# W_ada in bursts of four: regrouping the second part of a modulation inside a transformer block kernel

## The chip, the cores and the metric

The kernel runs on one core of a Trainium2 chip. The metric is the device time of one execution in microseconds, the median of several runs. Five engines work side by side in one core: PE (TensorE, matrix products; its weight loads are listed as PEld), DVE (VectorE), ACT (ScalarE), POOL (GpSimd) and SP (SyncE, which here issues every DMA). Each engine executes its own instructions in a fixed order, and they wait for each other through semaphores.

## The reference, cut to what matters

One block of a network over 1024 tokens of width 1024: a modulation, attention with dilated branches, a gated delta rule, an output projection, a feed-forward part and a last norm. The change touches the modulation alone, one row vector times a 1024x6144 matrix:

```python
c_act = jax.nn.silu(c)
mod = c_act @ w_ada[l] + b_ada[l]
sh1, sc1, g1, sh2, sc2, g2 = [m[:, None, :] for m in jnp.split(mod, 6, axis=-1)]
h = _rmsnorm(x, norm_attn_g[l]) * (1.0 + sc1) + sh1
...
x = x + g1 * y
h = _rmsnorm(x, norm_ffn_g[l]) * (1.0 + sc2) + sh2
...
x = x + g2 * y
```

sh1 and sc1, the first third, are needed at once, and the kernel computes them in its first stage. g1, sh2, sc2 and g2, the last two thirds, are not needed before the output projection. They are columns 2048 to 6143 of W_ada, 16 MB, and they are what the change is about.

## The kernel before, in words

**Stages.** First the norm, the first third of the modulation and six column blocks of the input projection (lines 156 to 500). Then the gated delta rule for two groups of four heads (`delta(0)`, `delta(1)`, lines 1165 to 1193), then attention (`attend`, 1310), the output projection (`out_delta`, 1335, and the loop at 1463), the feed-forward part and the last norm. The large products are made of three matmuls on numbers split in a high and a low part, 128x128 weights against 512 or 256 columns.

**Filler.** The delta rule is a chain of small steps that pass between PE, DVE, ACT and POOL. So that PE has work meanwhile, the rest of the input projection is a generator, `others()` (1106): each `yield` stands for a group of three matmuls and names their estimated time (0.64 or 0.32 us, lines 572 and 595). `turn(name)` (556) pulls as much filler as the table FILL (42) says ahead of a step; `until(...)` and `hold(...)` (1139 to 1147) pull until a named projection is done. `mixed()` (1126) wraps the generator: when more than MODS = 1.9 us of filler have gone by, and the flag `quiet` is not set (it is, in the triangular inverse of a group, line 943), it advances the modulation by one step.

**The modulation's last two thirds.** `modulation()` (1084) is a generator too. It goes through eight column groups `i` of 512 columns. For each of the eight row blocks `k` of 128 rows it takes a tile `wm` of 128x512 (256 KB), loads it from W_ada (1094), and calls `rows4` (191), which issues four matmuls: the column `cc[:, k:k+32]` as weights of 32 columns, and 128 strided columns of the tile as moving data, each into its own 32 partitions of the PSUM bank `mods`. In the records each of these four matmuls stands as two, so one tile is `x8` in a view. A column group takes a quarter (128 columns) of the bank; after its eight tiles, `by_columns` (201) lets DVE transpose the quarter into a tile `mt` (204) and add the bias into `mod` (208). The matmuls accumulate on what lies in the bank (`start=False`), so DVE clears the whole bank before group 0 and before group 4 (1090). There are 64 tiles in all, and a `yield` after each.

**Slots.** The tiles `wm` share the tag `tc` with two other users: `Rs`, three tiles in the first microseconds (183), and `tc_` in the triangular inverse (887), with TCB = 3 slots for all. A tile can be loaded when the tile that held the slot before is done with. The tiles `mt` share the two slots of the tag `zt` with the outputs of the z projection (612).

**Order.** The order of each engine's instructions is made by a planner before the run: it takes, on each engine, the instruction with the lowest place in the program among those whose inputs and slots are there by its own estimate. `urgent()` (93) puts an instruction 6000 places ahead; the loads of `wm` are written that way, as are the loads of the projection weights (`wsplit`, 210).

Of the kernel before, what the change touches and what calls it, by code (L numbers as in the profile page):

```python
# [10 lines left out]
F32 = mybir.dt.float32  # L11
# [7 lines left out]
P = 128  # L19
T = 1024  # L20
D = 1024
KT = D // P
TB = T // P
HALF = 512
# [2 lines left out]
SKEW = 4  # L27
TCB = 3
MODS = 1.9
EARLY = 1  # L30
LEVELS = ("qd", 4), ("z1", 36)
TAIL = 4
# [38 lines left out]
def build(tc, I, out):  # L71
    nc = tc.nc
# [3 lines left out]
    def pool(name, side="left", bufs=1, space=None):  # L76
        st = ExitStack()
        kw = {} if space is None else {"space": space}
        p = st.enter_context(
            tc.tile_pool(name=name, bufs=bufs, side=side, reuse_waits="tile", **kw)  # L80
        )
        return p, st
# [7 lines left out]
    def const(shape, name, dt=F32):  # L90
        return cp.tile(shape, dt, name=name, tag=name)

    def urgent():
        return tc.high_priority(offset=6000)
# [26 lines left out]
    pd, sd = pool("pd")  # L121
# [9 lines left out]
    def psb(name, tag, bufs):  # L131
        return pg.tile([P, HALF], F32, name=name, tag=tag, bufs=bufs)

    def gbank(name):
        return psb(name, "g", 2)
# [4 lines left out]
    def tbank(name):  # L140
        return psb(name, "t", 2)

    def abank(name):
        return psb(name, "a", 1)

    def ybank(name):
        return psb(name, "y", 1)

    def start(name, tag, shape=None, dt=F32):

        n = {"xp": 2, "qk": 4, "lu": 5, "o": 2, "VN": 2, "R": 1, "tc": TCB, "yt": 1, "os": 1, "zl": 1}.get(tag, 2)
        return pd.tile(shape or [P, T], dt, name=name, tag=tag, bufs=n)
# [3 lines left out]
    cc = const([P, KT + 31], "cc")  # L156
# [20 lines left out]
    for j in range(3):  # L177
        n = min(HALF, 1152 - HALF * j)
        ps = tbank(f"ps_R{j}")
# [11 lines left out]
    def rows4(ps, win, w, nt, last):  # L191

        v = w.rearrange("p (t j m) -> p j t m", j=4, m=32)
        for j in range(4):
            nc.tensor.matmul(
                ps[32 * j : 32 * j + 32, 0 : 32 * nt], win, v[:, j], start=False, stop=last, skip_group_check=True
            )

    def by_columns(ps, out, nt, add=None, shape=None, tag="os"):

        t = shape or start("turned", tag, [P, 256])
        nc.vector.transpose(t[:, 0 : 32 * nt], ps[:, 0 : 32 * nt])
        if add is None:
            nc.vector.tensor_copy(out, t[:, 0 : 32 * nt : 32])
        else:
            nc.vector.tensor_tensor(out=out, in0=t[:, 0 : 32 * nt : 32], in1=add, op=ALU.add)
# [207 lines left out]
    for i in range(2):  # L416
        ps = aux[:, P * i : P * i + P]
# [126 lines left out]
    def ahead(us):  # L544

        some = us > 0
        while us > 0:
            w = next(fill[0], None)
            if w is None:
                break  # L550
            us -= w
            used[0] += w
        return some and last[0] is not None
# [44 lines left out]
    def run(gen):  # L598
        for _w in gen:
            pass  # L600


    for q in range(2):
        ps = gbank(f"g_qd{q}")
# [478 lines left out]

    def modulation():
        pm = ybank("mods")
        for i in range(8):
            t0 = 16 + 4 * i
            ps = pm[:, P * (i % 4) : P * (i % 4 + 1)]
            if i % 4 == 0:
                nc.vector.memset(pm, 0.0)  # L1090
            for k in range(KT):
                w = pd.tile([P, HALF], F32, name=f"wm_{i}_{k}", tag="tc", bufs=TCB)
                with urgent():
                    nc.sync.dma_start(w, I["wada"][k * P : (k + 1) * P, t0 * P : t0 * P + HALF])
                rows4(ps, cc[:, k : k + 32], w, 4, k == KT - 1)
                yield
            t = pv.tile([P, 256], F32, name=f"mt{i}", tag="zt", bufs=2)
            by_columns(ps, mod[:, t0 : t0 + 4], 4, bada[:, t0 : t0 + 4], shape=t)
        nc.vector.scalar_tensor_tensor(
            out=G2, in0=mod[:, 32:40], scalar=1.0, in1=gff, op0=ALU.add, op1=ALU.mult  # L1100
        )

    done = set()
    mods = modulation()

    def others():
        def group1(which):
            for i, (kind, col) in enumerate((("kd", KD), ("qd", QD), ("vd", VD))):
                if kind in which:
                    for q in range(2):  # L1110
                        yield from proj_d(col + 2 + q, f"{kind}{2 + q}", spill(f"{kind}{q}", _.pj[2 * i + q]))
                    done.add(kind)

        yield from proj_t(I["wz0"], 256, "z0", z_evac(0))
        yield from group1(("kd", "qd", "vd"))
        yield from proj_t(I["wz1"], 256, "z1", z_evac(1))
        done.add("z1")
        for hp in range(4):
            if hp < 2:
                yield from proj_t(I["wva"][hp], 256, f"va{hp}", va_end(hp))  # L1120
                done.add(f"va{hp}")
            for col, kk in ((KA, 4), (QA, 0)):
                yield from proj_d(col + hp, f"a{kk}_{hp}", spill(f"a{kk}_{hp}", _.qk[kk + hp]))
            done.add(hp)

    def mixed():

        t = 0.0
        for c in others():
            yield c  # L1130
            t += c
            if t > MODS and not quiet[0]:
                t = 0.0
                next(mods, None)

    quiet = [False]
    fill[0] = mixed()

    def hold(what, us):
# [5 lines left out]
    def until(ready):  # L1145
        while not ready():
            used[0] += next(fill[0])
# [17 lines left out]
    def delta(g):  # L1165
        st = {}
        kt = []
        for j in range(4):
            kind, q = ("k", j) if j < 2 else ("q", j - 2)
            hp = 2 * g + q  # L1170
            t = pd.tile([P, T], F32, name=f"{kind}d{hp}", tag=f"{kind}d", bufs=2)
            (kd if kind == "k" else qd)[hp] = t
            if g == 0:
                conv((4 if kind == "k" else 0) + hp, xps[j], t)
                kt.append(delta_turn(g, kind, q, t, norms=norms[0], keep=kind == "k"))
                if j == 1:
                    nc.scalar.activation(norms[0]["lr"], norms[0]["rk"], AF.Ln, bias=eps1)
            else:
                nc.sync.dma_start(t, _.cv[j])
                if kind == "k":  # L1180
                    kt.append(delta_turn(g, kind, q, t, keep=True))
        delta_prep(g, st, norms[g], kt[0:2], delta_rows(g))
        if g == 1:
            until(lambda: "vd" in done)
        delta_v(g, st, [lambda q=q: vxp[q] if g == 0 else fetch(4 + q, f"v{2 + q}") for q in range(2)])
        delta_inverse(g, st)
        until(lambda: ("qd", "z1")[g] in done)
        delta_scan(g, st)
        if g == 0:
            delta_early()  # L1190

    delta(0)
    delta(1)
    until(lambda: EARLY - 1 in done)
    run(mods)
# [90 lines left out]
    def att_value(hp, qb, ets):  # L1286
# [12 lines left out]
        if qb % 4 == 3:  # L1299
            cs = slice((qb - 3) * P, (qb + 1) * P)  # L1300
            if hp < EARLY:
                t = pa.tile([P, HALF], F32, name=f"yo{hp}_{qb}", tag="xo", bufs=3)
# [7 lines left out]
    def attend(switch):  # L1310
        units = [(hp, qb) for hp in range(4) for qb in range(TB)]
        xs, ets = {}, {}
        for i in range(len(units) + AV):
            if i >= AV and units[i - AV] == (EARLY, 3):
                switch()
            if i < len(units):
                hp, qb = units[i]
                if hp not in loaded:
                    until(lambda: hp in done)
                    loaded[hp] = att_load(hp)  # L1320
                if i < EARLY * TB + 3 + AV:
                    ahead((FRONT - used[0]) / (EARLY * TB + 3 + AV - i))
                if qb >= 2 and hp < 3 and hp + 1 in done and hp + 1 not in loaded:
# [35 lines left out]
    def switch():  # L1359

        run(fill[0])
        sh_.close()
        p1_, st1 = pool("py", side="right")
        p2_, st2 = pool("pyd", side="right")
        closing.extend((st1, st2))
        for k in range(KT):
            p_ = p1_ if k < 4 else p2_
            yh[k] = p_.tile([P, T], F32R, name=f"yh{k}", tag=f"yh{k}")
            yl[k] = p_.tile([P, T], F32R, name=f"yl{k}", tag=f"yl{k}")
        for k in range(4, 8):  # L1370
            y_load(k, _.yd[k // 2 - 2][k % 2])
        fill[0] = out_delta()
# [3 lines left out]
    sy, syd = closing  # L1376
    for k in range(EARLY):
        y_load(k, _.ya[k])
    run(fill[0])

    ps = abank("g2t")
# [81 lines left out]
    for hf in range(2):  # L1463
# [4 lines left out]
        for d in range(KT):  # L1468
            slabs = [(wsplit(I["wo"][d, 0], 512, f"wo{d}_0_{hf}"), 0)]
            t = x2[d, hf]  # L1470
            nc.sync.dma_start(t, _.xp[2 * d + hf])
            ps = (gbank, sbank)[d % 2](f"wo{d}_0_{hf}")
# [204 lines left out]
    for k in range(4):  # L1677
# [3 lines left out]
        t = px.tile([P, HALF], F32, name=f"t2_{k}", tag="m", bufs=5)  # L1681
# [232 lines left out]
```

## Time and profile before

| what | value |
|---|---|
| median of 3 runs | 1443.23 us (1440.9 to 1454.74) |
| the profiled execution's own time | 1445.04 us |
| its span, from the first to the last instruction | 1443.3 us |
| PE busy in the span | 95% |
| DVE, ACT, POOL busy | 61%, 46%, 21% |
| mean granted clock of PE | 0.985 |
| loads of `wm`, line 1094 | 64 of 256 KB |

A row of the profile's groups or of its timeline names the time, the engine, the line of the kernel, the operation, the tile that is written, the tiles that are read, and the shape; `x8` counts instructions that follow each other. A matmul row shows its weights as `128*32` (rows and columns of the array) and its moving data as `128x128`. Matmuls are pipelined, and the ends of their bars are modelled: what one costs is read from the distance between starts. In brackets stands how long the engine was idle ahead of it and what ended that. A view by windows gives the busy time of each engine in a stretch of the span, with the granted clock of PE (PEclk, 1.00 is full) and what DMA moved.

### The profile page before, as it was taken

How to read it: one execution, taken by the hardware profiler on the slowest of the kernel's cores; microseconds unless marked ns; L12 is line 12 of the kernel's file. 1: busy time of each engine (PE TensorE's matmuls, PEld its weight loads, DVE VectorE, ACT ScalarE, POOL GpSimd, SP SyncE). 2: the span in 40 equal slices, each digit the busy share in tenths (PEclk: the TensorE clock that was granted, in tenths of full speed). 3: DMA queues.
4: the chain of work that ended last, by engine and by line, in shares of the span. 5: the costliest groups of instructions: out<-in, count | busy, mean ns of one | idle time of the engine just before them, and what ended most of it. 6: DMA issues, size and time to landing. Idle time of an engine off the chain costs nothing.

```text
span 1443.3 us, 24528 instructions
## 1 busy us (share of the span) xinstructions
PE 1372.5 (95%) x8984; PEld 1112.9 (77%) x8984; DVE 875.8 (61%) x1660; ACT 668.3 (46%) x1283; POOL 310.3 (21%) x279
## 2 busy tenths in 40 slices
PE   7998989997999699999998989999999999999997
PEld 4776857787879677777876868888888888888885
DVE  3587762665746223376426997757576776474487
ACT  3487523348233345576337743333333333444456
POOL 1345412243333334454244300000000000000000
PEclk9998999999999999999999999999999999999999
DMA  8736464466541643651375445636354565766666
GB/s 300 244 119 172 139 197 148 148 183 185 156 121 45 190 109 103 187 147 67 127 229 163 147 137 177 204 108 211 124 182 144 163 217 183 265 213 202 194 222 234
DMA packets 171921, 245.69 MB, mean 170 GB/s; under 512 B 33078, under 2 KB 76391, under 8 KB 171800
## 3 DMA queue, kind: packets, MB, share of 16 engines
q1 hardware_dynamic: 171800, 244.12, 54.4%
q8 instruction: 71, 1.16, 0.4%
q14 instruction: 50, 0.41, 0.1%
HBM read 181.30 MB, written 67.48 MB: 172 GB/s over the span
## 4 chain that ended last, share of the span: by engine, by line
PE 58%; DVE 6%; DMA 4%; ACT 2%; issue 1%; POOL 1%; SPq 0%; DVEq 0%; ACTq 0%; POOLq 0%
PE wua L1536 8%; PE wga L1536 8%; PE X L1731 6%; PE g_a L570 5%; PE wuc L1536 4%; PE Z L1731 4%; PE wgc L1536 4%; PE wo L570 3%; PE y L1295 2%; PE Y L1731 2%; PE tr L1278 2%; PE wgb L1536 2%; PE wub L1536 2%; PE g_va L593 2%; PE S L1254 1%
## 5 line engine op out<-in xcount | busy, mean ns | idle before, releaser
L1526 DVE TENSOR_TENSOR wl_db<-wr_db,wh_db 128x512 fp32r<-128x512 f32 x77 | 53.2, 691 | 76.4 <-ACT wh_db L1525 76.2
L1525 ACT CAST wh_db<-wr_db 128x512 fp32r<-128x512 f32 x77 | 47.9, 622 | 98.7 <-PE X L1731 41.3
L1258 DVE CUSTOM_DVE_ANT_0 X<-S,ng 128x512 f32<-128x512 f32 (+3 forms) x64 | 36.7, 587 | 71.5 <-PE S L1255 58.4
L1263 ACT ACTIVATE X<-X,sc 128x128 f32<-128x128 f32 (+7 forms) x64 | 49.4, 773 | 42.0 <-DVE sc L1258 36.6
L1731 PE MATMUL X<-wl_db,wh_da 128*128 128x512 f32 x176 | 68.6, 390 | 0.2 <-DVE wl_db L1526 0.2
L1731 PE MATMUL X<-wh_db,wh_da 128*128 128x512 f32 x176 | 68.6, 390 | 0.0
L1731 PE MATMUL X<-wh_db,wl_da 128*128 128x512 f32 x176 | 68.5, 389 | 0.0
L1265 POOL TENSOR_SCALAR X<-X,sc 128x128 f32<-128x128 f32 (+7 forms) x64 | 49.9, 782 | 82.3 <-DVE sc L1264 80.8
L1526 DVE TENSOR_TENSOR wl_da<-wr_da,wh_da 128x512 fp32r<-128x512 f32 x77 | 52.7, 686 | 1.2 <-ACT wh_da L1525 1.2
L570 PE MATMUL g_a<-hh,wh_a 128*128 128x512 f32 x128 | 53.2, 416 | 0.0
L570 PE MATMUL wo<-yh,wh_wo 128*128 128x512 f32 x128 | 51.5, 404 | 1.0 <-DVE xo L1346 1.0
L570 PE MATMUL wo<-yl,wh_wo 128*128 128x512 f32 x128 | 50.5, 394 | 0.9 <-DVE yl L1357 0.9
L570 PE MATMUL g_a<-hl,wh_a 128*128 128x512 f32 x128 | 51.0, 398 | 0.0
L570 PE MATMUL g_a<-hh,wl_a 128*128 128x512 f32 x128 | 50.7, 396 | 0.0
L570 PE MATMUL wo<-yh,wl_wo 128*128 128x512 f32 x128 | 50.6, 396 | 0.0
L1525 ACT CAST wh_da<-wr_da 128x512 fp32r<-128x512 f32 x77 | 47.3, 616 | 5.8 <-PE wua L1536 5.8
L1525 ACT CAST wh_wg_s<-wg_s 128x512 fp32r<-128x512 f32 x33 | 20.5, 622 | 55.4 <-PE wuc L1536 23.5
L1278 PE MATMUL tr<-ident,X 128*128 128x128 f32 x288 | 43.3, 277 | 2.8 <-DVE et L1281 1.8
L1254 PE MATMUL S<-KS,QS 128*128 128x512 f32 (+3 forms) x96 | 35.7, 380 | 10.2 <-ACT KS L1228 8.0
L217 POOL TENSOR_TENSOR wl_wo<-wr_wo,wh_wo 128x512 fp32r<-128x512 f32 x24 | 33.1, 1382 | 56.9 <-ACT wh_wo L216 55.9
L1295 PE MATMUL y<-et,va 128*64 128x128 f32 x576 | 42.8, 279 | 0.0
L1278 PEld LDWEIGHTS tr<-ident,X 128*128 128x128 f32 x288 | 33.0, 140 | 11.9 <-issue 4.6
(545 smaller groups left out, 4366.5 us busy)
## 6 DMA issues: line engine op xcount, KB each, us to landing
wr_da<-ao_d SPq DMA_DIRECT2D x77, 256.0 KB, 3.3
wm<-in_wada SPq DMA_DIRECT2D x64, 256.0 KB, 3.7
wr_wu<-in_wu SPq DMA_DIRECT2D x50, 256.0 KB, 2.9
wr_wg<-in_wg SPq DMA_DIRECT2D x48, 256.0 KB, 3.0
ao_d<-a SPq DMA_DIRECT2D x44, 256.0 KB, 2.7
wr_wd<-in_wdn SPq DMA_DIRECT2D x44, 256.0 KB, 3.1
wr_db<-wt_d SPq DMA_DIRECT2D x44, 256.0 KB, 3.0
ao_d<-as SPq DMA_DIRECT2D x33, 256.0 KB, 2.0
```

What stands on the lines that cost most here:

```text
L217: (eng or nc.gpsimd).tensor_tensor(out=lo[:, :n], in0=raw[:, :n], in1=hi[:, :n].bitcast(F32), op=ALU.subtract)
L570: last[0] = nc.tensor.matmul(ps, a[:, w0], b[k0 + k4][:, cs], start=(i == 0), stop=(i == n - 1))
L1254: nc.tensor.matmul(ps[:, 0 : c1 - c0], QS[:, qs], KS[:, c0:c1], start=True, stop=False)
L1258: nc.vector.tensor_tensor_reduce(out=X[:, c0:c1], in0=ps[:, 0 : c1 - c0], in1=ng[:, u + c0 : u + c1], scale=1.0, scalar=(3e38 if m is None ...
L1263: nc.scalar.activation(X[:, 0:nk], X[:, 0:nk], AF.Exp, scale=-1.0, bias=m, accum_out=sc[:, 2:3])
L1265: nc.gpsimd.tensor_scalar(out=X[:, 0:nk], in0=X[:, 0:nk], scalar1=sc[:, 3:4], scalar2=0.0, op0=ALU.mult, op1=ALU.add)
L1278: nc.tensor.transpose(ps[:, (kb - c0) * P : (kb - c0 + 1) * P], X[:, kb * P : kb * P + P], ident)
L1295: nc.tensor.matmul(yps[64 * e : 64 * e + 64, yc], va[:, kb, 64 * e : 64 * e + 64], ets[e][:, kb, :], start=(kb == 0), stop=(kb == qb),)
L1525: nc.scalar.copy(hi, src)
L1526: (eng or nc.vector).tensor_tensor(out=lo, in0=src, in1=hi.bitcast(F32), op=ALU.subtract)
L1536: nc.tensor.matmul(ps, a[:, w0], b, start=(first and k == 0 and n_ == 0), stop=(k == 3 and n_ == 2), skip_group_check=True,)
L1731: nc.tensor.matmul(bank[b], a[:, ts_], w, start=(first and f == 0 and n_ == 0), stop=(f == NF - 1 and n_ == 2), skip_group_check=True,)
```

## The change

The loop over `k` goes in steps of four. For each step four tiles are taken and loaded, then `rows4` is called for the four of them, and only then comes the `yield`. The tiles have a tag of their own, `wm`, with eight slots, instead of the three that they shared. The threshold in `mixed()` is four times as large, so four tiles come after every 7.6 us of filler where one came after 1.9. The bank is cleared as a whole once, at the start; after that, a quarter is cleared when it has been read, in the groups 0 to 3.

```diff
+BURST = 4
...
     def modulation():
         pm = ybank("mods")
+        nc.vector.memset(pm, 0.0)
         for i in range(8):
             t0 = 16 + 4 * i
             ps = pm[:, P * (i % 4) : P * (i % 4 + 1)]
-            if i % 4 == 0:
-                nc.vector.memset(pm, 0.0)
-            for k in range(KT):
-                w = pd.tile([P, HALF], F32, name=f"wm_{i}_{k}", tag="tc", bufs=TCB)
-                with urgent():
-                    nc.sync.dma_start(w, I["wada"][k * P : (k + 1) * P, t0 * P : t0 * P + HALF])
-                rows4(ps, cc[:, k : k + 32], w, 4, k == KT - 1)
+            for k0 in range(0, KT, BURST):
+                ws_ = []
+                for k in range(k0, k0 + BURST):
+                    w = pd.tile([P, HALF], F32, name=f"wm_{i}_{k}", tag="wm", bufs=2 * BURST)
+                    with urgent():
+                        nc.sync.dma_start(w, I["wada"][k * P : (k + 1) * P, t0 * P : t0 * P + HALF])
+                    ws_.append(w)
+                for k, w in enumerate(ws_, k0):
+                    rows4(ps, cc[:, k : k + 32], w, 4, k == KT - 1)
                 yield
             t = pv.tile([P, 256], F32, name=f"mt{i}", tag="zt", bufs=2)
             by_columns(ps, mod[:, t0 : t0 + 4], 4, bada[:, t0 : t0 + 4], shape=t)
+            if i < 4:
+                nc.vector.memset(ps, 0.0)
...
-            if t > MODS and not quiet[0]:
+            if t > BURST * MODS and not quiet[0]:
                 t = 0.0
                 next(mods, None)
```

## The prediction

> **What bounds the kernel now.** I read the page's first two parts, then the windows over the stretch in which the tiles `wm` are used, then the tile view of the bank `mods`, then the timeline of PE around single visits.
>
> ```profile
> span 1443.3 us, 24528 instructions
> PE 1372.5 (95%) x8984; PEld 1112.9 (77%) x8984; DVE 875.8 (61%) x1660; ACT 668.3 (46%) x1283; POOL 310.3 (21%) x279
> ```
>
> ```profile
> core 0: us, PE busy (x) PEld busy (x) DVE busy (x) ACT busy (x) POOL busy (x), PEclk, DMA share, GB/s
> 138.95:146.50 7.55, 7.55 (x51) 7.14 (x48) 2.85 (x6) 6.38 (x20) 3.21 (x2) 0.50 0.56 167
> 306.00:355.00 49.00, 41.02 (x381) 35.49 (x381) 30.65 (x46) 38.55 (x72) 15.50 (x12) 0.93 0.71 210
> 118.00:401.00 283.00, 262.77 (x2421) 211.98 (x2420) 174.76 (x351) 128.49 (x260) 99.55 (x88) 0.96 0.58 169
> ```
>
> ```profile
> L197 PE MATMUL mods<-wm,cc x512: 272/297/423, 118.6 to 396.4; 128*32 128x128 f32 x171
> ```
>
> PE bounds the kernel as a whole, and the stretch of the change too: between 118 and 401 us PE is idle for 20 of 283 us. So an instruction taken off PE there shortens the kernel, unless the stretch ends on another engine. One piece looks like that: from 306 to 355 us PE is idle for 8 of 49 us.
>
> **First part: fewer visits.** 64 tiles are 64 visits of PE to the narrow matmuls; afterwards there are 16. One visit:
>
> ```profile
> 173.64 0.39 PE L570 MATMUL g_kd<-hh,wl_kd 128*128 128x512 f32 x1
> 173.96 0.42 PE L197 MATMUL mods<-wm,cc 128*32 128x128 f32 x8
> 174.32 0.50 PE L570 MATMUL g_kd<-hh,wh_kd 128*128 128x512 f32 x1
> 174.65 0.39 PE L570 MATMUL g_kd<-hl,wh_kd 128*128 128x512 f32 x1
> 174.88 0.39 PE L570 MATMUL g_kd<-hh,wl_kd 128*128 128x512 f32 x1
> 176.59 0.32 PE L197 MATMUL mods<-wm,cc 128*32 128x128 f32 x4
> ```
>
> From one visit to the next are 176.59 - 173.96 = 2.63 us, and nine wide matmuls lie between. They go in steps of 0.23 us (174.65 to 174.88), so nine take 2.07 us, and the visit costs 2.63 - 2.07 = 0.56 us. It is not only the eight records: 0.32 us pass ahead of the first (0.09 over the usual step) and 0.33 us from the first wide matmul behind to the second (0.10 over). What does a tile cost that follows another one? The first stage has eight tiles in a row:
>
> ```profile
> 52.68 1.97 PE L197 MATMUL sums<-wm,cc 128*32 128x128 f32 x64
> 54.57 0.50 PE L237 MATMUL f<-hh,wh_f 128*128 128x512 f32 x1
> ```
>
> Eight tiles take 1.89 us up to the next wide matmul, one takes 0.36 (173.96 to 174.32). A further tile costs (1.89 - 0.36) / 7 = 0.22 us. Four visits of today cost 2.24 us, a visit with four tiles 0.56 + 3 x 0.22 = 1.22. Sixteen times the difference of 1.02 is 16.3 us of PE. I count it in full where PE is the bound and not at all where the next step waits for another engine. There are two such places, with two of the sixteen bursts in each: before `trq` at 138.95 (next part), and between 306 and 355 us, where PE's waits are for DVE and ACT:
>
> ```profile
> PE kk_k L779 <- DVE qk L785: 3.0, 2, 2.6
> PE trq_0False L717 <- ACT cv L537: 2.3, 1, 2.3
> PE ps_bp L760 <- DVE nbp L754: 1.8, 1, 1.8
> ```
>
> Four bursts of 1.02 us are 4.1 us not seen. This part: -12.2 us; its ends are -16.3 (all seen) and -6.6 (only a solid run of projection matmuls, some 69 us from 168 to 237 us, in which at 2.63 us a visit 26 tiles or 6.5 bursts lie).
>
> **Second part: eight slots.** With three slots a load waits for the visit three tiles earlier. Once that stops PE:
>
> ```profile
> 132.87 0.42 PE L197 MATMUL mods<-wm,cc 128*32 128x128 f32 x8
> 135.88 0.43 PE L197 MATMUL mods<-wm,cc 128*32 128x128 f32 x8 [2.58 <-DMA wm<-in_wada]
> 138.37 0.66 PE L197 MATMUL mods<-wm,cc 128*32 128x128 f32 x8 [2.06 <-DMA wm<-in_wada]
> 138.95 1.12 PE L717 MATMUL trq_0False<-ident,qd 128*128 128x128 f32 x4
> ```
>
> Three tiles stand behind each other, and 4.64 us go by with PE idle. With eight slots of their own all eight tiles of the first column group can be in long before. The stall goes; what is late next? `trq` needs the convolution that ACT ends at 134.3; behind it ACT squares it and then takes the 64 exponentials `dt`, which need `lr`, last written by DVE at 138.1:
>
> ```profile
> 133.23 1.06 ACT L537 ACTIVATE qd<-qd 128x1024 f32<-128x1024 f32 x1 [1.65 <-DVE qd L533]
> 140.10 0.60 ACT L723 ACTIVATE sqq<-trq_0False 128x512 f32<-128x512 f32 x1 [3.79 <-PE trq_0False L717]
> 140.60 0.97 ACT L750 ACTIVATE dt<-dt,lr 128x128 f32<-128x128 f32 x3
> ```
>
> ```profile
> 137.92 0.17 DVE L747 TENSOR_TENSOR lr<-lr,Gc 128x32 f32<-128x32 f32 x1
> ```
>
> ACT can start at 138.1 + 0.1 instead of 140.6. I take 2.4 us, not 4.64, because the products that follow are multiplied by `dt`. The ends are 0 and 4.64 plus half of the 7.55 us in which, right behind the stall, PE ran at a granted clock of 0.50 (3.8 us more).
>
> The Trainium skill, "TensorE: Matmul & The Clock Gate", section "HAM oscillation — how this bites in real kernels", says that a pause of PE over about 3.4 us halves its clock, so that taking the pause away keeps it full. By that rule the second part would be -6.2 us, by the row alone it is -2.4. The trace agrees that the halving follows the two pauses; that the time behind is PE's and not ACT's no row shows.
>
> The same slots also took loads away from the inverse (`tc_`); nothing on PE waits for those tiles long, so I take 0. On SP four loads now stand in one piece behind one burst, about 4 x 0.45 us of issuing; what follows on SP are weight loads written ahead in the same way, so I take 0, which would be some 2 us if a weight load came late.
>
> **Third part: the start.** The loads are placed 6000 instructions ahead, and only slots hold them back. Today that is visible: the first three go out as soon as `Rs` has left its slots.
>
> ```profile
> 0.80 0.39 SPq L166 DMA_DIRECT2D wa<-in_wa  x1
> 1.40 0.33 SPq L158 DMA_DIRECT2D cc<-in_cc  x1
> 9.00 2.35 SPq L185 DMA_DIRECT2D R_d<-Rs  x3
> 11.90 1.36 SPq L1094 DMA_DIRECT2D wm<-in_wada  x3
> ```
>
> ```profile
> 3.92 1.28 ACT L159 ACT_TABLE_LOAD   x1 [3.92 <-DMA cc<-in_cc]
> ```
>
> ```profile
> 8.00:12.00 4.00, 3.20 (x19) 0.75 (x17) 2.03 (x7) 2.00 (x3) 0.35 (x1) 1.00 0.33 110
> 12.00:36.00 24.00, 21.74 (x143) 14.63 (x144) 7.96 (x13) 9.09 (x14) 4.99 (x4) 0.93 0.99 370
> ```
>
> The new slots have had no owner, so nothing holds the first eight loads: I expect them as SP's first DMAs, ahead of `wa` and `cc`. Eight issues of 0.45 us (1.36 us for three) put `cc` 3.6 us later; 2.1 MB at the 370 GB/s of the stretch 12 to 36 us are 5.7 us of transfers. The first work of ACT and PE waits for `cc`. Against that, three loads leave at 11.9 us, and DMA is idle for two thirds of 8 to 12 us. From 12 to 36 us DMA is full, and 1.3 MB more in all are 3.5 us there. Ends: 0 (hidden behind the idle stretch) and +5.7; I take +4, near both 3.6 and 3.5.
>
> The Trainium skill, "DMA: Bandwidth & Descriptors", section "Queues, rings and completion order", says that each DMA engine takes the descriptors of a ring in their order. By that rule `cc` waits for the whole 2.1 MB, and the term is +5.7. No run here shows it yet; it speaks against the change.
>
> **Fourth part: clearing by quarters.** Before, two clears of the whole bank; after, one and four of a quarter:
>
> ```profile
> L1090 DVE MEMSET mods<- 128x512 f32 x2 | 1.0, 485 | 0.2
> L399 DVE MEMSET sums<- 128x128 f32 x1 | 0.2, 165 | 0.4 <-ACT rs L389 0.4
> ```
>
> On DVE that is 4 x 0.165 - 0.485 = +0.2 us. It matters where PE waits for it: the next burst writes the bank that DVE reads and now also clears. Once DVE is late:
>
> ```profile
> 191.06 0.65 PE L197 MATMUL mods<-wm,cc 128*32 128x128 f32 x8 [3.89 <-DVE mt L204]
> ```
>
> ```profile
> 169.91 1.10 DVE L865 TENSOR_TENSOR tm<-nt,tt 128x31 f32<-128x31 f32 x1
> 190.69 0.31 DVE L204 STREAM_TRANSPOSE mt<-mods 128x128 f32<-128x128 f32 x1
> 199.60 0.19 DVE L869 TENSOR_TENSOR tt<-tt,tm 128x31 f32<-128x31 f32 x1
> ```
>
> DVE is in the triangular inverse from 169.91 to 199.8 us, and the transpose `mt` stands in its middle. Behind this wait the rest of the projection `kd` queues on PE. After the change the second column group ends 5.8 us of filler later, still inside the inverse; both PE and DVE come there later by about the same. I let the wait stand and add 0.5 us for the clears; its ends are -4 (the group ends behind the inverse) and +9 (199.8 less 191).
>
> **The sum.** -12.2 - 2.4 + 4.0 + 0.5 = -10.1 us on the profiled execution's own 1445.04 us (1.7 over its span) gives 1435. The median of the runs lies 1.8 below that execution, so I predict 1433 us.
>
> **The rivals.** (a) Everything counts: the 16.3 us are all seen, the stall gives 4.6, the start costs nothing, or the clock stays full: 1443.2 - 16.3 - 4.6 = 1422, and 1418 with 3.8 us for the clock. For it: PE idles in only 20 of 283 us. Against it: ACT and DVE are what comes late at 139 and within 306 to 355 us. The clock rule quoted above belongs here. (b) The bursts aren't what they seem: the planner may put steps of the chain between the tiles of a burst, or the delta chain, not PE, sets the end of each stage. Then perhaps 5 us remain, and the start takes 4 of them: 1442. For it, a tile that stands in two pieces today, with other work between them:
>
> ```profile
> 121.28 0.41 PE L197 MATMUL mods<-wm,cc 128*32 128x128 f32 x2
> ```
>
> Against it, inside the projection runs all eight records stand together. (c) Slower: DVE's transpose and clear get placed behind the inverse. PE then stands from about 187 to 200 us, 13 us in place of 3.9, its clock drops as it did at 138.95 (3.8 us), and with the start at +5.7 the sum is -12.2 - 2.4 + 5.7 + 9 + 3.8 = +3.9: 1447; with the first part at its low end of -6.6 it is 1453. It decides as soon as that wait passes 9 us. For it: one such wait exists; against it, the next transposes find DVE free.
>
> **How the numbers follow.** My forecast, from 1426 to 1439, has 0.46; (a) 0.25; (b) 0.20; (c) 0.09. One per cent, about what a measurement of this kernel can tell from no change, is 1428.8 and 1457.7. Faster takes all of (a) and 0.07 of the forecast's lower edge: 0.32. Slower takes the part of (c) in which the wait is longer still or comes twice: 0.04. The rest is 0.64. The range, 1419 to 1447, leaves out the lowest and the highest tenth.
>
> **What would show it.** In the timeline after: visits of `x32` with about 1.0 us to the next wide matmul; no idle time before `mods` for a DMA; SP's first eight DMAs from line 1094, and ACT's first work near 8 us, not 3.92; PE's wait for `mt` between 3 and 5 us around 190. If ACT's first work stays at 3.9, the third part is wrong; if bursts stand apart as `x8`, the first; if the stage from 306 to 355 us ends earlier by more than the stage before it did, the places where I count nothing were wrong.

## The result, and the profile after

The changed kernel takes 1438.39 us (median of 15 runs, 1434.07 to 1460.88); the kernel before, run beside it, 1445.37 us (15 runs, 1440.9 to 1454.74). The ratio is 0.9948 with a 95% interval of 0.9929 to 0.9968. The profiled execution took 1435.81 us against 1445.04. All ratios below leave disturbed runs out, and each is against the kernel before in runs on the same chip, because its median moves from one set of runs to the next (1445.4 to 1449.4). By the ratio the change is worth some 7.5 us.

First the page: the span, and each engine's busy time.

```profile
span 1434.1 us, 24528 instructions
PE 1353.0 (94%) x8984; PEld 1113.6 (78%) x8984; DVE 879.5 (61%) x1663; ACT 663.0 (46%) x1279; POOL 309.9 (22%) x279
```

PE's busy time fell by 19.5 us (1372.5 to 1353.0) and the span by 9.2. So PE has less to do, as meant, and it stands idle more. The timeline of PE after shows a burst, and with it what a visit costs:

```profile
191.05 1.08 PE L198 MATMUL mods<-wm,cc 128*32 128x128 f32 x32
192.06 0.50 PE L571 MATMUL g_kd<-hh,wh_kd 128*128 128x512 f32 x1
...
200.44 1.08 PE L198 MATMUL mods<-wm,cc 128*32 128x128 f32 x32
```

The 32 records of four tiles stand together, and 1.01 us pass to the next wide matmul. From burst to burst are 9.39 us with 36 wide matmuls, at 0.23 us each 8.28: a burst costs 1.11 us. Counted in the timeline, PE goes to these matmuls 25 times; before, 70 times. Eleven of the sixteen bursts stand in one piece. The planner broke the other five, which lie among steps of the delta rule, into fourteen pieces; one of them begins like this, with matmuls of the chain in between:

```profile
266.67 0.41 PE L198 MATMUL mods<-wm,cc 128*32 128x128 f32 x2
...
268.50 0.43 PE L198 MATMUL mods<-wm,cc 128*32 128x128 f32 x8
```

PE's waits after, and then before, from 85 to 450 us (total, times, longest):

```profile
PE trv L837 <- ACT vd L538: 12.5, 2, 11.9
PE kk_q L780 <- DMA qd<-cv_d: 2.5, 1, 2.5
PE trq_0False L718 <- ACT qd L538: 2.1, 1, 2.1
...
PE g_z L594 <- ACT zt L615: 1.6, 1, 1.6
```

```profile
PE mods L197 <- DMA wm<-in_wada: 5.5, 3, 2.6
PE mods L197 <- DVE mt L204: 4.7, 3, 3.9
...
PE trv L836 <- ACT vd L537: 1.1, 1, 1.1
```

Of the two waits of `mods` only 0.7 us are left, for a clear. A new one stands at its top: 11.9 us ahead of `trv`, the transposes of the value rows in the second group. The windows over that place, 331 to 365 us, after, and the windows from 300 to 445 us, before and after:

```profile
331.00:365.00 34.00, 20.36 (x166) 19.31 (x167) 28.54 (x40) 9.43 (x14) 15.45 (x14) 0.75 0.34 101
```

```profile
300.00:445.00 145.00, 134.64 (x1427) 114.73 (x1427) 83.72 (x164) 69.44 (x140) 48.92 (x44) 0.98 0.53 154
```

```profile
300.00:445.00 145.00, 126.04 (x1391) 112.28 (x1390) 89.00 (x175) 58.96 (x128) 47.21 (x39) 0.94 0.44 131
```

After, PE is idle for 13.6 of the 34 us, at a mean granted clock of 0.75. In the 145 us its idle time grew from 10.4 to 19.0 us. Followed by the last start of a tile on PE, the lead over the kernel before is:

| tile, last start (first, where said) | before, us | after, us | lead, us |
|---|---|---|---|
| `ps_GT`, first | 116.6 | 118.2 | -1.6 |
| `ps_bp`, first | 140.7 | 139.6 | 1.1 |
| `g_kd` | 204.0 | 194.7 | 9.3 |
| `g_vd` | 307.4 | 293.7 | 13.7 |
| `kk_k` | 350.9 | 330.6 | 20.3 |
| `mods` | 396.4 | 388.8 | 7.6 |
| `X`, the last matmuls of the kernel | 1433.9 | 1425.0 | 8.9 |

The change had won 20 us by 331 us and gave 13 back by 389. Behind that the lead changes by little more than 1 us.

**Why PE stands before `trv`.** This is the timeline of ACT, after, and then of the kernel before at the same step:

```profile
321.13 7.71 ACT L751 ACTIVATE dt<-dt,lr 128x128 f32<-128x128 f32 x26
328.74 1.05 ACT L819 ACTIVATE eb<-eb 128x1024 f32<-128x1024 f32 x1
329.68 1.15 ACT L532 ACTIVATE vd<-xp_v,cw 128x1024 f32<-128x1024 f32 x1
...
340.38 1.28 ACT L538 ACT_TABLE_LOAD   x1 [4.89 <-DVE vd L534]
341.68 1.06 ACT L538 ACTIVATE vd<-vd 128x1024 f32<-128x1024 f32 x1
```

```profile
326.73 1.15 ACT L531 ACTIVATE vd<-xp_v,cw 128x1024 f32<-128x1024 f32 x1 [1.64 <-DMA xp_v<-pj_d]
...
338.74 7.12 ACT L750 ACTIVATE dt<-dt,lr 128x128 f32<-128x128 f32 x24
...
347.18 0.38 ACT L614 ACTIVATE zt<-g_z 128x256 f32<-128x256 f32 x1
...
355.60 1.06 ACT L537 ACTIVATE vd<-vd 128x1024 f32<-128x1024 f32 x1
```

`vd` is the convolution of the values, and PE needs it for `trv`. It has a first step on ACT, then steps on DVE, then a last step on ACT. `zt` takes a finished tile of the z projection, which is filler, out of PSUM. Two things are different. Before, the first step of `vd` stands at 326.73 us, ahead of the exponentials `dt`; after, it stands behind them, at 329.68, and ACT then waits 4.89 us for DVE's steps. And before, two `zt` (at 347.18 and 350.58) come ahead of the last step of `vd`, so the z filler goes on while `vd` is made; after, no `zt` comes between `dt` and `vd`. PE has neither `vd` nor filler from 331 to 342.8 us. The diff touches none of these steps. Only the planner's order is another one.

### The profile page after: what moved, and what is told of

The parts are those of the page before. It is cut to its first block, busy times and chain, and to the rows that moved or that the text cites. A ratio compares the mean times of both kernels' runs of the same rounds, so it can differ in the third digit from the quotient of the medians.

```text
span 1434.1 us, 24528 instructions
## 1 busy us (share of the span) xinstructions
PE 1353.0 (94%) x8984; PEld 1113.6 (78%) x8984; DVE 879.5 (61%) x1663; ACT 663.0 (46%) x1279; POOL 309.9 (22%) x279
## 4 chain that ended last, share of the span: by engine, by line
PE 71%; DVE 12%; DMA 8%; ACT 4%; issue 3%; POOL 1%; SPq 1%; DVEq 0%; ACTq 0%; POOLq 0%
PE wua L1542 8%; PE wga L1542 8%; PE X L1737 6%; PE g_a L571 6%; PE wuc L1542 4%; PE Z L1737 4%; PE wgc L1542 4%; PE wo L571 3%; PE Y L1737 2%; PE y L1301 2%; PE f L238 2%; PE tr L1284 2%; PE wgb L1542 2%; PE wub L1542 2%; PE g_va L594 2%
```

## The experiments

The theory: what the change saves is visits, at some 0.33 us each (1.22 us a burst against 4 x 0.56), and it comes through in full; 13 us of it are lost because the planner, given another program around it, puts ACT's work for the second group in another order. Rivals: the slots bring the gain; the early loads or the clears take it; the delta chain, not PE, sets the end of each stage, so that PE's time was never worth much. The edits are to the changed kernel.

**1. The slots alone.** One tile a visit, eight slots.

```diff
-BURST = 4
+BURST = 1
-    tag="wm", bufs=2 * BURST
+    tag="wm", bufs=8
```

> One tile per visit again, with eight slots of its own and the clears by quarters. Theory 1 (a visit costs 0.56 us of PE, a tile that follows another 0.22): the 64 visits are back, so nearly all of the gain goes; what stays is the stall before `trq` near 133 us (about -2.7 us at that place) and the later start (+1.6 us at 118 us): 1 to 3 us below the kernel before. Rival 2 (the gain comes from the slots, not from the visits): about as fast as the changed kernel, 7 to 9 us below the kernel before. For the loss between 306 and 355 us: if loads issued four in a row cause it, it is gone here; if the order that the planner makes of ACT's work there causes it, it is smaller here, since ACT's order now has two more z outputs ahead of the exponentials `dt`.

Measured: 1454.56 us, ratio 1.0043 (1.0024 to 1.0063), 62 visits. The slots alone bring no gain, so the rival that they do is out; they even cost 0.43%, and PE idles 28.9 us from 85 to 450 us where it idled 23.5 before. From here to the changed kernel (1.0043 to 0.9948) are 0.95%, some 13.7 us, for 37 visits: 12.2 us at 0.33. PE's idle time doesn't explain this gap: in the changed kernel it is 29.4 us, about the same as here. The waits of PE show what one tile a visit keeps:

```profile
PE g_va L594 <- ACT zt L615: 8.5, 1, 8.5
PE mods L198 <- DVE mods L1104: 4.8, 2, 4.5
```

The wait for DVE between two column groups is here (4.5 us, now for the quarter's clear), and so is one of 3.2 us for `mt` in the second group. A wait of 8.5 us for ACT stands in the second group too, at another tile.

**2. The first eight loads not ahead.**

```diff
-                    with urgent():
+                    with urgent() if i > 0 else ExitStack():
                         nc.sync.dma_start(w, ...)
```

> The changed kernel with the loads of the first column group at their place in the program instead of 6000 instructions ahead, so that the start has none of them. If the eight loads at the start are a cost, ACT's first work is back at 3.9 us and everything from 118 us on is 1.6 us earlier than in the changed kernel (between 1 and 2 in the median); a price of 4 us, as predicted, would be 4 earlier at 118 us. Rival: the loads are hidden, and nothing moves by 118 us. The order of ACT's work between 306 and 355 us is the same as in the changed kernel, so the long wait of PE for `vd` there stays, near 12 us.

Measured: 1433.33 us, ratio 0.9906 (0.987 to 0.9942). In the timelines of SP and ACT of the changed kernel the loads are SP's first, and ACT begins at 9.90 us; here ACT begins at 3.89:

```profile
0.80 3.71 SPq L1096 DMA_DIRECT2D wm<-in_wada  x8
4.63 0.52 SPq L159 DMA_DIRECT2D cc<-in_cc  x1
```

```profile
9.90 1.28 ACT L160 ACT_TABLE_LOAD   x1 [9.90 <-DMA cc<-in_cc]
```

```profile
3.89 1.28 ACT L160 ACT_TABLE_LOAD   x1 [3.89 <-DMA cc<-in_cc]
```

`ps_GT` starts at 115.0 us here, at 118.2 in the changed kernel and at 116.6 in the one before, which had three of these loads early itself. So at that point the eight loads cost 3.2 us against none and 1.6 against before; the expectation had 1.6 against none. The gain at the end is larger still (4.5 us at the last `X` of the profiled executions, 0.42% by the ratios). Part of that is the clock: behind `ps_GT` the changed kernel has 3.4 us at half clock (below), and this run has none there. The wait for `trv` stays, 10.4 us.

**3. Four slots.**

```diff
-    tag="wm", bufs=2 * BURST
+    tag="wm", bufs=BURST
```

> The changed kernel with four slots instead of eight: a burst's loads can be issued only when the burst before is done. The bursts are 9.4 us apart in the projection runs and a load lands in some 4 us, so if eight slots are more than is needed PE waits for no load and the time is that of the changed kernel, less about half of the 1.6 us of the start. If depth matters, PE waits for DMA ahead of `mods` at several of the sixteen bursts, 1 to 3 us each, and the kernel is 5 us or more slower than the changed one.

Measured: 1444.26 us, ratio 0.9975 (0.9953 to 0.9997). A burst must now be read before the next can be loaded, and PE's waits get a line that the changed kernel doesn't have:

```profile
PE mods L198 <- DMA wm<-in_wada: 6.7, 12, 3.1
```

So with bursts the loads come late in four slots. What that costs in all is less clear: the ratio's interval overlaps with the changed kernel's. In the profiled executions `ps_GT` is 2.4 us earlier than in the changed kernel (115.8 us) and the last `X` 3.4 us later (1428.4).

**4. The convolution of v first, in group 1.**

```diff
+            with urgent() if g == 1 else ExitStack():
-            conv(8 + hp, vps[q](), vd)
+                conv(8 + hp, vps[q](), vd)
```

> The changed kernel with the convolution of v in the second group (`vd`) placed ahead in the planner's order, so that ACT and DVE do it before the exponentials `dt` and not after them. If the order of ACT's work makes PE's wait of 11.9 us before `trv` (the lost 14 us between 306 and 355 us), that wait falls under 3 us and the kernel is 8 to 14 us faster than the changed one, 15 to 22 below the kernel before. If the cause is the four loads in a row on SP, which stay, or the half clock, the wait stays near 12 us and the time within 2 us of the changed kernel.

Measured: 1437.49 us, ratio 0.9923 (0.989 to 0.9957). The wait for `trv` fell from 11.9 to 1.4 us, as the theory says. The time did not follow: the interval overlaps with the changed kernel's, and 8 us or more were expected. The profiled execution took 1450.69 us, because of a stretch at half clock that the last section shows. Behind that stretch it is 18.9 us late against the changed kernel (last `g_vd`); 12.5 us of this are back by the last `g_z`, and 6 are lost again by the last `lx` (444 us), with a wait of 4.8 us of `g_a` for ACT's copy `sp_a`. So the order makes the wait for `trv`, but what is pulled ahead on ACT seems to push something else back.

**5 and 6. Bursts of eight, and of two.** Eight slots in both; bursts of eight with sixteen slots were not run.

```diff
-BURST = 4
+BURST = 8        (e5_b8)    or    BURST = 2        (e6_b2)
-    tag="wm", bufs=2 * BURST
+    tag="wm", bufs=BURST    (e5_b8)    or    bufs=8    (e6_b2)
```

> Bursts of eight tiles in the same eight slots, a column group per visit: 8 visits. By the price of a visit (0.56 us, and 0.22 for each tile that follows) a burst takes 2.1 us and comes every 72 x 0.23 + 2.1 = 18.7 us in the projection runs; that is 2.7 us of PE less than in the changed kernel. The loads of a burst can go out only when the one before is done, 18 us ahead: no wait for a load. If a visit's cost grew with its length (the weights of 32 columns as the bound), a burst would take 8 x 0.36 = 2.9 us or more and the step would be 19.4. In ACT's order three more z outputs stand ahead of the exponentials `dt` than in the changed kernel, so if that order makes PE's wait before `trv`, the wait is under 6 us here and the kernel 5 to 12 us faster than the changed one; if not, 2 to 3 us.

> Bursts of two tiles in eight slots: 32 visits. By the price of a visit the step in the projection runs is 18 x 0.23 + 0.78 = 4.92 us (a rival with no saving per visit: 5.25, twice the 2.63 of single tiles). PE has 5.4 us more than with bursts of four. The wait for DVE's `mt` inside the inverse (4.8 us with single tiles in eight slots, none with four) should be between: a burst leaves DVE 4.9 us instead of 2.6, so 1 to 3 us. The whole kernel: between the single tiles in eight slots and the changed kernel, ratio to the kernel before about 0.998 to 1.002.

Measured: bursts of eight 1459.3 us, ratio 1.0081 (1.0049 to 1.0113), with 7 visits; bursts of two 1459.11 us, ratio 1.0066 (1.0047 to 1.0085), with 40 visits. Both miss. For the eight, the wait for `trv` is short as the theory says (2.6 us), but other waits are new. The timelines of SP and ACT:

```profile
207.12 0.32 SPq L873 DMA_DIRECT2D tn_d<-tt  x1
...
207.97 0.72 SPq L1072 DMA_DIRECT2D pj_d<-sp_kd  x1
...
228.89 6.24 SPq L1096 DMA_DIRECT2D wm<-in_wada  x8
235.39 0.33 SPq L1072 DMA_DIRECT2D pj_d<-sp_kd  x1
```

```profile
211.40 0.37 ACT L1071 COPY sp_kd<-g_kd 128x256 f32<-128x256 f32 x1 [10.64 <-DMA pj_d<-sp_kd]
...
240.29 0.78 ACT L1071 COPY sp_qd<-g_qd 128x256 f32<-128x256 f32 x2 [13.72 <-DMA pj_d<-sp_kd]
```

With as many slots as tiles in a burst, the eight loads stand on SP until the burst ahead is read, and the store `pj_d` at 235.39 us stands behind them. ACT's copy out of PSUM waits 13.7 us for a store to free its buffer, and PE waits for ACT. The copy's wait of 10.6 us ahead of 211.40 has another cause: there SP stands 8.1 us at `tn_d`, which needs the end of DVE's inverse, and the store follows at 207.97. In the waits of PE:

```profile
PE trq_0False L718 <- ACT qd L538: 7.1, 1, 7.1
PE mods L198 <- DMA wm<-in_wada: 6.8, 9, 3.5
PE g_qd L571 <- ACT sp_qd L1071: 6.0, 1, 6.0
PE g_qd L571 <- ACT sp_kd L1071: 4.9, 1, 4.9
```

The second and the third, 12.8 us, come of slots and loads; 18 visits fewer than with bursts of four save only 6. The fourth belongs to the copy behind `tn_d`. The first is once more ACT's order: `eb`, for whose load ACT waits 1.94 us, stands ahead of `qd`.

For the two, the visit is as expected: a burst costs 4.92 us from start to start (206.02 to 210.94) with 18 wide matmuls, so 0.78 us. But this execution has a stretch of 51 us at half clock:

```profile
406.40:457.60 51.20, 50.32 (x537) 42.28 (x537) 15.47 (x38) 13.77 (x35) 7.08 (x8) 0.50 0.14 41
```

The work from the last `mods` to the last `lx` takes 62.1 us in it, 42.9 in the changed kernel: 19 us. Its timed executions all have a mean clock of 0.968 to 0.973 (the profiled one of the changed kernel has 0.985), so this stretch, or one like it, seems to be in each. Without these 19 us its ratio would be near 0.993, an estimate.

**7. The bank cleared as a whole.** The first clear goes back into the loop, at `i % 4 == 0`, and the clears by quarters go.

```diff
-        nc.vector.memset(pm, 0.0)
         for i in range(8):
+            if i % 4 == 0:
+                nc.vector.memset(pm, 0.0)
...
-            if i < 4:
-                nc.vector.memset(ps, 0.0)
```

> The changed kernel with the clears of before: the whole bank ahead of the column groups 0 and 4, no quarters. On DVE that is 0.2 us less. If the quarters cost PE anything, it is in the wait ahead of the bursts that open a column group (1.1 us at 172 us in the changed kernel): 0.2 us less there, and nothing in the total (within 1 us of the changed kernel). Rival: the clear of the whole bank ahead of group 4 has to wait for the read of group 3 and PE for it, which costs the 0.5 us of the clear once.

Measured: 1443.11 us, ratio 0.9977 (0.9942 to 1.0012). The interval overlaps with the changed kernel's, so the times don't tell the two apart. The profiled execution has 41 us at half clock from 233.7 us; ahead of that it is the changed kernel's (last `g_qd` 219.7 against 220.0 us), and the wait for `trv` is there (11.6 us). PE's wait of 0.7 us for a quarter's clear is gone; more than that the clears don't show.

**8 and 11. One more filler ahead of `trv`.** The table FILL gets one entry, which makes 10.24 us of filler in front of `trv2_0`; without the early loads (8) and with them (11).

```diff
     "trv3_0": 10.24,
+    "trv2_0": 10.24,
```

> Two edits on the changed kernel: the first column group's loads at their place in the program (as before, some 3 us at the start), and 10.24 us of filler ordered ahead of the first transpose `trv` of the second group, so that PE has the z projection to do while ACT and DVE make `vd`. If PE's wait of 10 to 12 us there is work that was ordered too late, the wait falls under 4 us, the window at half clock behind it goes or shrinks, and the kernel is 6 to 12 us faster than with the late loads alone, about 0.984 to 0.987 of the kernel before. Rival: the work is only moved, and the same time is lost before the triangular inverse or its block steps, where PE then has less filler left: within 3 us of the kernel with late loads alone.

> The changed kernel with the one entry added to the list of fillers, its first eight loads ahead as in the changed kernel. If the eight loads cost 3 us and the filler gains 8 us, apart from each other (theory): ratio 0.986 to 0.989, first work of ACT at 11 us, ps_GT 3 us later than in e8_zfill (114.0) and that lag kept to the end. If the lag is taken up again by waits behind it (rival): ratio 0.983 to 0.985.

Measured: 8 takes 1425.26 us, ratio 0.9842 (0.9802 to 0.9881), the best of all. 11 takes 1430.44 us, ratio 0.9896 (0.9861 to 0.9931). The windows from 300 to 445 us of 8, to hold against the two rows above, and the wait for `trv` in 8 (it is 4.0 us in 11):

```profile
300.00:445.00 145.00, 136.22 (x1462) 121.54 (x1462) 94.11 (x206) 61.46 (x138) 49.23 (x43) 0.98 0.45 128
```

```profile
PE trv L838 <- ACT vd L539: 5.0, 1, 5.0
```

PE's idle time is 8.8 us, not 19.0. In 8 the first step of `vd` still stands behind the exponentials `dt` (325.78 us); what PE has again is filler, which the order had taken away. The wait was expected under 4 us and is 5.0; the time is within what was expected. Four kernels make a square: with the loads ahead 0.9948 and, with the filler, 0.9896; without the early loads 0.9906 and 0.9842. The filler is worth 0.52% and 0.64% (7.5 to 9 us), the start 0.42% and 0.54% (6 to 8 us). Each of these differences is uncertain by some 0.4 to 0.5%, so they are only just clear of noise. The profiled executions agree: at the last `X` the filler is worth 5.6 and 6.2 us, the start 4.5 and 5.1, and as far as these four tell the two effects hardly touch each other. Experiment 11 started later than the changed kernel (`cc` ready at 10.91 us) and was 7.7 us behind 8 at `ps_GT`, where 3 were expected.

**9 and 10. One tile, and two, on that version.** Both have eight slots, no early loads and the new filler.

```diff
-BURST = 4
+BURST = 1        (e9_ones_z)    or    BURST = 2        (e10_twos_z)
-    tag="wm", bufs=2 * BURST
+    tag="wm", bufs=8
```

> One tile a visit (BURST = 1) with eight slots, the first column group not placed ahead, and the list of fillers as in e8_zfill, whose ratio was 0.984. If a visit costs PE 0.33 us and nothing else differs (theory), some 40 more visits than in e8_zfill's 28 cost 13 us: ratio 0.993, between 0.990 and 0.997, with g_kd last about 9 us later than e8_zfill's 190.1. If the planner's order or windows at half clock decide and the visits count little (rival), the ratio is 0.984 to 0.988 or, with a new window of 40 us or more, over 1.0, and the trace shows that window.

> Bursts of two with eight slots on the version of e8_zfill. Bursts of two on the changed kernel gave 1.0066, with 51.2 us at half clock from 406.4 us in the profiled execution. If that window was the whole of the surprise (theory), this version costs about 14 visits of 0.33 us more than e8_zfill, 5 us: ratio 0.987 to 0.990, and no window of 40 us or more. If bursts of two are themselves bad, say through the order that the planner makes of them (rival), the ratio is 0.995 or more without such a window.

Measured: one tile 1450.95 us, ratio 1.0016 (0.9994 to 1.0038), 65 visits; two tiles 1442.53 us, ratio 0.9973 (0.9951 to 0.9995), 39 visits. Both are slower than the price of the visits says, though neither has a long stretch at half clock. For some nine of the missing microseconds the rival is right. The wait of PE with one tile (with two it is 9.2 us):

```profile
PE g_va L595 <- ACT zt L616: 9.3, 1, 9.3
```

The kind of wait that the filler had cured comes back at another tile: the order has put `zt` behind the second `vd` on ACT, and PE's filler has no bank to write. With one tile, the last `X` starts 26.2 us later than in 8 (1440.5 against 1414.3). 37 visits more at 0.33 us are 12.2. The wait for the quarter's clear (4.5) and this one (9.3) are new, and shorter waits of 8 are gone: PE's whole idle time from 85 to 450 us grows by 9.4 (19.6 to 29.0). Together that is 21.6. The time at half clock in the same window is 34.1 us, 17.1 in 8, and by PE's busy time in it I estimate some 6 us from that. With two, visits (3.6) and this wait make 12.8 of 15.0.

## Why the prediction was right, step by step

The time is 5 us above the 1433, within the range. On the profiled execution the sum of -10.1 us stands against -9.2 measured; by the medians it is -7.0. The price of a visit and the mechanism of the start were right; that the sum came out is in part luck, because gains and a loss that no part had, more than 10 us on either side, took each other away. Part by part:

- **First part, visits (-12.2).** The price was right: 1.22 us a burst forecast, 1.11 measured; the whole time of experiment 1 fits with 12 us for 37 visits, and that of 9 with it and two more terms. The count was 48 visits fewer, and 45 came, because five bursts were broken. The places where it was not to count were wrong. I had left out the bursts from 306 to 355 us because PE waits for DVE and ACT there. The stage gained all the same: the lead grew from 13.7 to 20.3 us between `g_vd` and `kk_k`. Up to `kk_k` the gain behind `ps_bp` is 19.2 us: 29 visits fewer are 9.6, the wait for `mt` 3.9, the waits of `kk_k` (2.6) and `trq` (2.3) in the list of before are gone and one of `kk_q` (2.5) is new. That makes 15.9. The other 3 us are the clock. The kernel before has two stretches of 3.4 us at half clock here, behind its waits of 3.89 us for `mt` and of 2.30 us ahead of `trq`, in which PE is busy; by the granted clock of 0.50 I estimate that full clock would save half of each, 1.7 us. The changed kernel has none from 146 to 333 us. The first of the two, in the kernel before, and the second:

```profile
191.00:194.30 3.30, 3.24 (x14) 2.36 (x15) 3.09 (x10) 0.00 (x0) 0.00 (x0) 0.50 0.44 106
```

```profile
330.95:334.35 3.40, 3.40 (x19) 3.40 (x18) 2.56 (x3) 3.37 (x8) 0.38 (x1) 0.51 0.98 319
```

- **Second part, slots (-2.4).** The lead grew by 2.7 us from `ps_GT` to `ps_bp`. The slots alone are not measured by that: four visits fewer (1.3 us) are in it, and 3.4 us at half clock that the kernel before doesn't have there. No load stops PE any more; `trq` waits 2.11 us for ACT's `qd`, as forecast that something of ACT's would be late next. The rule of the clock in the Trainium skill, "TensorE: Matmul & The Clock Gate", section "HAM oscillation — how this bites in real kernels", had made it -6.2, and the row decides against it: the pause is shorter, 2.11 us, and the clock is at half speed behind it all the same, for 6.8 us where it was 10.2 (window 138.7 to 145.5 us). The kernel before spoke against it already: neither of its pauses, 2.58 and 2.06 us, is over 3.4 us, and the clock fell at some 136.3 us, behind the first and ahead of the second, not behind the two as the prediction reads it.

```profile
138.70:145.50 6.80, 6.02 (x41) 5.65 (x40) 4.21 (x12) 6.79 (x23) 3.78 (x2) 0.50 0.75 214
```

- **Third part, start (+4.0).** The mechanism came as said, and ACT's first work came later than said: 9.90 us, not 8. It is 5.98 us later than before. The Trainium skill, "DMA: Bandwidth & Descriptors", section "Queues, rings and completion order", holds that an engine takes a ring's descriptors in their order, by which it would be 5.7: the trace agrees. Of the 6 us, 1.6 were left at `ps_GT`, so the +4.0 was too much there. Against no early loads at all the start costs 3.2 us there and 0.4 to 0.5% of the time.
- **Fourth part, "I let the wait stand".** This step failed, to the good. After, PE waits 0.7 us at 172, for the clear, and not at all at 191. I had moved the second column group's end and left the spacing as it was. But with bursts, the next group's first tiles come 9.39 us after the last tiles of the group, not 2.63; in that time DVE did the transpose (188.33) and the clear (189.03) between two steps of its inverse:

```profile
188.33 0.31 DVE L205 STREAM_TRANSPOSE mt<-mods 128x128 f32<-128x128 f32 x1
188.56 0.37 DVE L866 TENSOR_TENSOR tm<-nt,tt 128x247 f32<-128x247 f32 x1
189.03 0.17 DVE L1104 MEMSET mods<- 128x128 f32 x1
```

With one tile a visit the wait is there, 4.5 us (1 and 9): the burst removes it, not the slots.
- **What no part had.** The order of the second group. With its long wait the lead fell by 13 us between `kk_k` and the last `mods`, and that made the sum right by accident: the wait of 3.9 us, the visits at 306 to 355 us and the stretches at half clock brought more than forecast, the order less. Rival (b) says that the planner may put steps of the chain between the tiles of a burst. That happened to five bursts of sixteen, and nine visits more cost some 3 us; what cost the most, another order of ACT's work, it does not name, though there too the chain and not PE sets the time. Rival (a), 1418 to 1422, needs the wait gone and the start free: experiment 11, which cuts the wait to 4.0 us and keeps the early loads, comes to 0.9896, by the 1445.37 of the kernel before 1430 us; experiment 8, without the early loads, to 0.9842 or 1422.5 us. Rival (c) did not come.

## What to carry to other kernels

Price a regrouping by the visit, from the distance between starts in the timeline; that price held within 10% in the timeline, and the time of the whole kernel fits it within a few us. Where a planner orders the instructions, an edit to the filler's spacing can reorder other engines: look for the largest new wait in the kernel after, ask whether the same work has lost its filler, and add filler at that point before judging the change. Look at what stands on a queue behind loads that wait for a slot: in experiment 5 a store stopped there, and the copy that needed its buffer waited 13.7 us.

## What the runs showed of the hardware

**Stretches at half clock behind short pauses.** In experiments 4 and 7, PE's granted clock falls to 0.50 for 41 us in the first group of the delta rule, behind a wait of 2.04 and 2.03 us ahead of `lw`; in 6 for 51 us (above). In experiment 8, the wait at the same place is 1.51 us and the clock stays at 1.00. The waits in the timelines of PE of 7 and 8, and the windows of 7 and 8:

```profile
232.32 1.14 PE L927 MATMUL lw<-tc,dt 64*64 64x64 f32 x16 [2.03 <-ACT tc L919]
```

```profile
228.12 1.14 PE L928 MATMUL lw<-tc,dt 64*64 64x64 f32 x16 [1.51 <-ACT tc L920]
```

```profile
233.70:274.70 41.00, 41.00 (x405) 31.51 (x404) 14.24 (x27) 10.62 (x24) 8.55 (x11) 0.50 0.21 59
```

```profile
228.00:276.00 48.00, 47.66 (x608) 39.24 (x608) 29.79 (x83) 18.18 (x47) 16.63 (x20) 1.00 0.42 123
```

From the first `lx` to the last `g_vd`, such a stretch costs 15.7 us (75.6 in experiment 7, 59.9 in the changed kernel), more than the change brings. The pause alone does not set its length: 11.9 us of wait ahead of `trv` are in a stretch of 17.1 us. Nor does it decide whether the clock falls at all. Ahead of `ps_GT` PE waits 1.96 us in the kernel before and 1.95 us in the changed kernel, and the clock behind it is full in the one, half in the other (windows before, then after); behind the changed kernel's wait of 2.53 us ahead of `kk_q` it is full too.

```profile
116.60:120.00 3.40, 3.40 (x33) 3.07 (x34) 2.03 (x4) 2.80 (x6) 0.00 (x0) 1.00 0.23 81
```

```profile
118.25:121.66 3.41, 3.41 (x17) 3.41 (x18) 1.99 (x4) 2.81 (x6) 0.00 (x0) 0.50 0.24 79
```

What decides it, and what sets the length, stays open. In the long stretch of experiment 7 the profile has PE busy throughout (41.00 of 41.00 us), so idle time of PE inside it is not what keeps the clock low.
